# A weight ring with four double places: pairs of pieces in one 2 MB load, the rest in single places of 1 MB

## The chip, the cores and the metric

One core of one Trainium2 chip. The time is device microseconds of one execution of the whole program; the kernel before takes 1867.7 us (median of 3 runs, 1866.82 to 1869.79). "MB" of a weight piece below is 1024 KB, as in the profile's list of DMA issues; the profile's own sums of MB and its GB/s are decimal.

## The reference

A decoder block over 512 tokens of width 1024: a mixer (a state-space branch and a pooling branch, gated and merged), then a mixture of 32 experts of which every token takes four. The change touches the weights of the experts only. What an expert computes for its tokens:

```
def expert_block(args):
    xblk, e = args
    gu = xblk @ w_gu[e] + b_gu[e]
    glu, lin = jnp.split(gu, 2, axis=-1)
    glu = jnp.minimum(glu, SWIGLU_LIMIT)
    lin = jnp.clip(lin, -SWIGLU_LIMIT, SWIGLU_LIMIT)
    act = glu * jax.nn.sigmoid(SWIGLU_ALPHA * glu) * (lin + 1.0)
    return act @ w_down[e] + b_down[e]
```

`w_gu[e]` is 1024 x 2048 and `w_down[e]` 1024 x 1024 in f32: 8 MB and 4 MB of weights for each of 32 experts, each read once.

## The kernel before

The mixer runs until about 712 us, the experts from there to about 1846 us, and a short norm ends the program. The experts are taken in ranks of their token count, in an order that a host function (`order_of_ranks`) writes down; below, u is the place in that order. Experts with few tokens (u = 1, 2, then the even u from 4 to 24, and 30, 31) are "half": their products (`products`, L1106) multiply the raw weights (8 matmul records a piece in the trace). The others are "full": ACT and DVE split each half piece into a high and a low part (`esplit`, which calls the split at L117 and L118) and PE makes 6 matmuls of each half piece, 12 of a piece (L1111 to L1113).

The main loop (before the last lines printed below) does for each u: `up(u)`, the eight pieces of `w_gu`, and then `down(u-1)`, the four pieces of `w_down` of the expert before; biases, the activation's rows and their transposes, the gather of the next tokens' rows and the scatter of results (POOL) hang on hooks between the pieces. So from u = 4 to u = 25 a repeating cycle is: `up` of a half expert, `down` of a full one, `up` of a full one, `down` of a half one.

Each piece is 1 MB and comes by one DMA that SP issues (`fetch`, L771). `fetch` takes the first name of the list `ring`, allocates the next tile of that name and puts the name back at the end: a first-in first-out ring, with 11 places of 1 MB in the steady state (S0 S1 S4 S5 r0 r1 r2 Z bc0 S8 r4). Several of the places also serve the mixer before and the last norm after. SP takes its DMAs strictly in order: a load whose place is still being read stops SP, and all later loads with it, until the last reader (PE for a half expert, the splits on ACT and DVE for a full one) is done. The scheduler that orders the instructions may hoist a load as early on SP as its order allows. The host hands over `wgu` and `wdn`; a piece of `wgu` has runs of 8 KB in a partition, one of `wdn` two runs of 4 KB. The number of each expert is read from a table by `value_load` (L757, on SP).

Of the kernel before, what the change touches and what calls it, by code (L numbers as in the profile page):

```python
# [9 lines left out]
F32 = mybir.dt.float32  # L10
# [10 lines left out]
P = 128  # L21
D = 1024
# [4 lines left out]
NE = 32  # L27
# [41 lines left out]
def hybrid_block(ctx: ExitStack, tc: tile.TileContext, cst, cols, rows, xt, xf, wad0, wada, bada,  # L69
                 wx, wz, wdt, wu, wg, wso, wpl, wpo, wo, wr, ball, wgu, wdn, out):  # L70
    nc = tc.nc
    V, S, G, TE, SP = nc.vector, nc.scalar, nc.gpsimd, nc.tensor, nc.sync
    sb = ctx.enter_context(tc.tile_pool(name="sb", bufs=1))
    pm = ctx.enter_context(tc.tile_pool(name="pm", bufs=4, space=PSUM))
    dr = ctx.enter_context(tc.tile_pool(name="dr", bufs=1, space=DRAM))
    uid = [0]


    shared = dict(t1=0, t2=512, dt=1024, ac=1152, dte=1280, eac=1408, cdk=1536, cwh=1664, tri=1784)
    Z = sb.tile([P, 2048], F32, tag="Z", name="Z")  # L80

    def T_(tag, cols_, dt=F32, parts=P):
        if tag in shared:
            o = shared[tag]
            return Z[0:parts, o:o + cols_]
        uid[0] += 1
        return sb.tile([parts, cols_], dt, tag=tag, name=f"{tag}_{uid[0]}")

    def bank(tag="mm"):
        uid[0] += 1  # L90
        return pm.tile([P, 512], F32, tag=tag, name=f"{tag}_{uid[0]}")
# [233 lines left out]
    dt, negA, a2 = T_("dt", P), T_("negA", NH), T_("a2", 2 * P)  # L325
# [376 lines left out]
    for jj in range(4):  # L702
        whi, wlo = load_split(wg[4 + jj])
        for j in (2 * jj, 2 * jj + 1):
            t = gate(whi, wlo, j % 2)
# [22 lines left out]
    for j in range(KD):  # L728
        if j % 2 == 0:
            whi, wlo = load_split(wg[j // 2])  # L730
        t = gate(whi, wlo, j % 2)
# [9 lines left out]


    def weights(e):
        def of(w, lo_, hi_):
            return w[e, lo_:hi_, :] if isinstance(e, int) else w[bass.ds(e, 1), lo_:hi_, :].squeeze(0)

        return dict(wu=lambda k: of(wgu, k * P, (k + 1) * P), got={},
                    wd=lambda c: of(wdn, c * 256, (c + 1) * 256).rearrange("(k p) d -> p k d", p=P))

    order = order_of_ranks()  # L750
    big = order.index(NE - 1)
# [6 lines left out]
        return wts[u]  # L758


    ring, kept = ["bc0", "S4", "S5", "r0", "r1", "r2", "S7", "r3"], ["Z", "bc0", "S8", "r4"]
    nload = [0, 0]
    wsp = []

    def fetch(w, kind, k, t=None):
        if t is None:
            t = ring.pop(0)
            if t not in ("S7", "r3", "S3"):
                ring.append(t)
        r = T_(t, 2048)  # L770
        SP.dma_start(r if kind == "wu" else r.rearrange("p (k d) -> p k d", k=2), w[kind](k))  # L771
        return r

    def eload(w, kind, k):
        return w["got"].pop((kind, k), None) or fetch(w, kind, k)

    def esplit(r):
        if not wsp:
# [16 lines left out]
    ss2, r2 = T_("ss2", 2 * NB), T_("rst", NB)  # L795
# [50 lines left out]
    for n in range(2):  # L846
# [6 lines left out]
        for b in range(NB):  # L853
# [9 lines left out]
            t = xg_rot()  # L863
# [342 lines left out]

    def warm():
        S.activation(rf[0:64, 0:1], parts[0][0][1][0][:, 0:1].bitcast(F32), AF.Sqrt, scale=0.0, bias=eps1[0:64, :])
        f = T_(ring.pop(3), D)
        fin.extend([f[:, 0:512], f[:, 512:D]])  # L1210
        for n in range(2):
            dg, ps = g_rot(), bank("ss")
            for k in range(4):
                f = Q_FN + n * 4 + k
                V.tensor_scalar(dg[:, k * P:(k + 1) * P], ident, qc[:, f:f + 1], None, op0=ALU.mult)
            TE.matmul(ps, ones, dg, start=True, stop=True)
            S.activation(fin[n], ps, AF.Copy)
# [117 lines left out]
    turn_routing()  # L1335
    first_rows()
    fetch_down(2, 4)
    ring[:] = ["S0", "S1", "S3", "S4", "S5", "r0", "r1", "r2", "r3"]
    ahead.append(list(pieces(weights_of(0)["got"]["wu", 1], True)))
    xe2 = []  # L1340

# [8 lines left out]
    prev, parts, pend, begin = None, [], [], []  # L1350
    for u in range(NE + 1):
        hooks = {}
        if u < NE:
            w, sel = weights_of(u), sel_of(u)
            pre = {k: list(f) for k, f in extra.get(u, {}).items()}
            if u != 0:
                pre.setdefault(0, []).append(lambda: prep(u + 2))
            if u == big - 2:
                pre.setdefault(4, []).append(prep_x)
            if pend:  # L1360
                pre[1] = pend + pre.get(1, [])
                pend = []
            for n, f in enumerate(begin):
                pre[n] = [f] + pre.get(n, [])
            begin = []
            pss = up(xs_[u], sel, w, pre)
            aTs = [op_of(Rot(["q16"]) if u == 1 else a_rot, xs_[u][0].half)]
            hooks = {n: [f] for n, f in enumerate(acts(pss[0], aTs[0]))}
            if u == big:
                aTs.append(op_of(Rot(["b12"]), True))  # L1370
                lx = act_rows(*pss[1])
                hooks[0].insert(0, lambda: act_turn(lx, aTs[1], 0))
            hooks[2] = hooks.get(2, []) + [lambda: turned(u + 1)]
            if u >= FIXED:
                hooks[0] = hooks.get(0, []) + [lambda: select(u + 1)]
            if u == big - 1:
                hooks[3] = hooks.get(3, []) + [turned_x]
        if u == NE:
            hooks = {0: [warm, lambda: open_sums(0, 3)], 1: [lambda: open_sums(3, 5)], 2: [lambda: open_sums(5, 7)]}
        if prev is None:  # L1380
            ls = [act_rows(pss[0][n], pss[0][n + 2]) for n in range(2)]
            begin = [lambda n=n, l=l, a=aTs[0]: act_turn(l, a, n) for n, l in enumerate(ls)]
            turned(1)
        else:
            v, aT0 = prev
            if v == 0:
                ring.extend(kept)
            psd = down(aT0, sel_of(v), weights_of(v), hooks)
            if u >= NE - 1:
                parts.append(spread(psd[0], sts[v]))  # L1390
            else:
                send(psd[0], sts[v])
                if len(psd) > 1:
                    pend.append(lambda p=psd[1]: send(p, sts["x"], "q16"))
        if u < NE:
            prev = (u, aTs)

    t0t = [T_(ring.pop(0), 2048) for _ in range(2)]
    t0 = [t0t[b // 2][:, (b % 2) * D:(b % 2 + 1) * D] for b in range(NB)]
    for b in range(NB):  # L1400
        SP.dma_start(t0[b], y_d[b * P:(b + 1) * P, :])
# [26 lines left out]
    with tc.For_i(0, nov, 1) as i:  # L1428
        w = tabled(bass.ds(i, 1))
# [4 lines left out]
        x = turn(st, x_rot)  # L1434
# [40 lines left out]
def _layout(i):  # L1475
    A = np.ascontiguousarray

    def tiles(w):
        return w.reshape(KD, P, w.shape[1] // P, P).transpose(2, 1, 0, 3)

    def pairs(t):
        return t.reshape(-1, 2, P, 1024).transpose(0, 2, 1, 3).reshape(-1, P, 2048)

    def halves(w):
        n = w.shape[1] // 512
        return w.reshape(2, 4, P, n, 512).transpose(3, 0, 2, 1, 4).reshape(n, 2, P, 2048)

    x, w_in = i["x"][0], i["w_in"][0]
    fcol = lambda v: v.reshape(-1, P).T
    cols = np.concatenate([  # L1490
        i["conv_w"][0].reshape(4, 24, P).transpose(2, 1, 0).reshape(P, 96), fcol(i["conv_b"][0]),
        fcol(i["ssd_norm_w"][0]), fcol(i["pool_scale"][0]), fcol(i["norm_mix_w"][0]), fcol(i["c"][0]),
        fcol(i["norm_ffn_w"][0]), fcol(np.repeat(i["d_skip"][0], 64)),
        fcol(i["norm_final_w"]), fcol(i["b_ada"][0][:2048]).reshape(P, 2, 4, 2).transpose(0, 2, 1, 3).reshape(P, 16)], axis=1)
    rows = np.concatenate([i["a_log"][0], i["dt_bias"][0], i["b_router"][0]])
    order = [t for g in range(4) for t in (16 + g, 20 + g, 4 * g, 4 * g + 1, 4 * g + 2, 4 * g + 3)]
    d = dict(
        cst=_consts(), cols=A(cols), rows=rows,
        xt=A(x), xf=A(x.T.reshape(2, 4, P, T).transpose(0, 2, 1, 3).reshape(2, P, 2048)),
        wad0=A(i["w_ada"][0][:, :2048].reshape(2, 4, P, 2, 4, 256).transpose(4, 0, 2, 1, 3, 5).reshape(4, 2, P, 2048)), wada=A(halves(i["w_ada"][0][:, 2048:])), bada=A(i["b_ada"][0].reshape(12, 512)),  # L1500
        wx=A(pairs(tiles(w_in[:, 2048:5120])[order])),
        wz=A(pairs(tiles(w_in[:, 0:2048]))),
        wdt=A(w_in[:, 5120:5152].reshape(KD, P, NH).transpose(1, 0, 2).reshape(P, 256)),
        wu=A(pairs(tiles(w_in[:, 5152:6176]))),
        wg=A(pairs(tiles(w_in[:, 6176:8224]))),
        wso=A(i["w_ssd_out"][0].reshape(4, 4, P, 2, 4, P).transpose(0, 3, 2, 4, 1, 5).reshape(8, P, 2048)),
        wpl=A(i["w_pool"][0].reshape(4, 2, P, 256).transpose(2, 0, 1, 3).reshape(P, 2048)),
        wpo=A(pairs(tiles(i["w_pool_out"][0]))),
        wo=A(halves(i["w_out"][0]).reshape(4, P, 2048)),
        wr=A(i["w_router"][0].reshape(KD, P, NE).transpose(1, 0, 2).reshape(P, 256)),  # L1510
        ball=A(np.concatenate([i["b_gu"][0], i["b_down"][0]], axis=1).reshape(NE, 3, 2, 512).transpose(2, 0, 1, 3).reshape(2, NE, 1536)),
        wgu=A(i["w_gu"][0]), wdn=A(i["w_down"][0]))
    return d


# [17 lines left out]
```

## Time and profile before

| | |
|---|---|
| median of 3 runs | 1867.7 us (1866.82 to 1869.79) |
| the profiled execution, its own time | 1870.85 us |
| its span | 1869.1 us |
| granted TensorE clock, mean | 0.989 |
| PE busy | 1788.1 us, 96% of the span |
| HBM read | 502.89 MB |

The span is the time from the first to the last instruction of that one execution; the own time also holds what lies around it. PE is the engine that is nearly always busy; the question for a change of the loads is whether they still come before PE wants them.

### The profile page before, as it was taken

Reading aid. Unit: us, or ns where it says so; the run is one execution under the profiler, and the core shown is the slowest. Engines: PE = TensorE matmul, PEld = TensorE weight load, DVE = VectorE, ACT = ScalarE, POOL = GpSimd, SP = SyncE. Lnnn points to the kernel's source line nnn. Section 1 sums busy time; section 2 is a strip of 40 time slices with the busy share of each in tenths; the row PEclk is TensorE's granted clock in tenths of the full one; section 3 lists DMA queues with packets and bytes.
Section 4 is the critical chain, followed back from the end, with each engine's and each line's share of the span. In section 5 each row is a group of like instructions: output and inputs, shape, how many; then the busy total and the mean of one; then the engine's idle time right before and its main releaser. Section 6 shows DMA issues by size and latency. Waiting matters only on the chain. (4 is left out here: it accounts for less than half of the span.)

```text
span 1869.1 us, 23339 instructions
## 1 busy us (share of the span) xinstructions
PE 1788.1 (96%) x8353; PEld 1165.1 (62%) x8353; DVE 1213.9 (65%) x1803; ACT 947.0 (51%) x1458; POOL 220.0 (12%) x214
## 2 busy tenths in 40 slices
PE   6999999999999999999999999999999999999995
PEld 3787687867768777456456455455564565677741
DVE  5888685857574548657557566375675585799933
ACT  4433545536362346346455455264555455577822
POOL 0000000010100002121111111121112111211111
PEclk9999999999999999999999999999999999999998
DMA  8265233352443458999999998789999999989894
GB/s 349 76 251 221 90 135 113 113 134 93 124 130 136 178 218 296 371 402 400 388 373 402 380 366 326 305 309 373 382 402 377 380 403 364 397 327 341 316 365 191
DMA packets 102728, 527.81 MB, mean 282 GB/s; under 512 B 11737, under 2 KB 12377, under 8 KB 60368
## 3 DMA queue, kind: packets, MB, share of 16 engines
q1 hardware_dynamic: 90544, 498.14, 68.8%
q0 software_dynamic: 11184, 25.50, 6.4%
q10 hardware_dynamic: 880, 2.64, 0.4%
q8 instruction: 67, 1.10, 0.2%
q14 instruction: 53, 0.43, 0.1%
HBM read 502.89 MB, written 25.77 MB: 283 GB/s over the span
## 5 line engine op out<-in xcount | busy, mean ns | idle before, releaser
L118 DVE TENSOR_TENSOR wl<-r,wh 128x1024 fp32r<-128x1024 f32 x246 | 303.6, 1260 | 109.4 <-ACT wh L117 100.2
L117 ACT ACTIVATE wh<-r 128x1024 fp32r<-128x1024 f32 x246 | 253.9, 1057 | 136.3 <-PE mm L266 56.2
L118 DVE TENSOR_TENSOR wl<-S,wh 128x1024 fp32r<-128x1024 f32 x186 | 229.8, 1271 | 34.3 <-ACT wh L117 34.1
L1112 PE MATMUL mm<-wl,S 128*128 128x512 f32 x540 | 217.3, 402 | 9.7 <-DVE wl L118 9.0
L1113 PE MATMUL mm<-wh,S 128*128 128x512 f32 x540 | 214.5, 397 | 0.0
L117 ACT ACTIVATE wh<-S 128x1024 fp32r<-128x1024 f32 x186 | 189.5, 1055 | 47.5 <-PE mm L1113 34.9
L265 PE MATMUL mm<-S,wh 128*128 128x512 f32 x512 | 207.9, 407 | 4.0 <-ACT S L117 4.0
L267 PE MATMUL mm<-S,wl 128*128 128x512 f32 x512 | 206.3, 403 | 1.5 <-DVE wl L118 1.5
L266 PE MATMUL mm<-S,wh 128*128 128x512 f32 x512 | 206.5, 403 | 0.0
L1111 PE MATMUL mm<-wh,S 128*128 128x512 f32 x540 | 177.7, 402 | 8.0 <-ACT wh L117 8.0
L1147 DVE TENSOR_SCALAR q<-mm 128x512 f32<-128x512 f32 x49 | 32.9, 687 | 181.8 <-PE mm L1106 153.1
L1148 ACT ACTIVATE q<-q 128x512 f32<-128x512 f32 x50 | 31.3, 632 | 218.0 <-DVE q L1147 217.8
L1112 PEld LDWEIGHTS mm<-wl,S 128*128 128x128 f32 x540 | 102.2, 189 | 47.6 <-DVE wl L118 17.0
L1111 PEld LDWEIGHTS mm<-wh,S 128*128 128x128 f32 x540 | 100.6, 188 | 48.7 <-ACT wh L117 16.3
L265 PEld LDWEIGHTS mm<-S,wh 128*128 128x128 f32 x512 | 97.2, 190 | 33.0 <-issue 7.1
L1113 PEld LDWEIGHTS mm<-wh,S 128*128 128x128 f32 x540 | 102.4, 190 | 21.5
L267 PEld LDWEIGHTS mm<-S,wl 128*128 128x128 f32 x512 | 97.0, 190 | 29.7 <-issue 6.4
L266 PEld LDWEIGHTS mm<-S,wh 128*128 128x128 f32 x512 | 97.3, 190 | 26.9 <-issue 4.2
L1112 PE MATMUL ss<-wl,S 128*128 128x512 f32 x240 | 97.1, 405 | 1.9 <-DVE wl L118 1.5
L1106 PE MATMUL mm<-S,S 128*64 128x512 f32 x408 | 96.2, 596 | 0.0
L1172 POOL TENSOR_TENSOR y<-y,q 128x512 f32<-128x512 f32 x47 | 67.7, 1453 | 237.9 <-ACT y L1171 237.2
L1113 PE MATMUL ss<-wh,S 128*128 128x512 f32 x240 | 95.5, 398 | 0.0
(499 smaller groups left out, 3101.2 us busy)
## 6 DMA issues: line engine op xcount, KB each, us to landing
S<-in_wgu SPq DMA_DIRECT2D x113, 1024.0 KB, 9.6
r<-in_wgu SPq DMA_DIRECT2D x97, 1024.0 KB, 8.4
S<-in_wdn SPq DMA_DIRECT2D x61, 1024.0 KB, 11.7
r<-in_wdn SPq DMA_DIRECT2D x44, 1024.0 KB, 13.2
bc<-in_wgu SPq DMA_DIRECT2D x23, 1024.0 KB, 10.3
Z<-in_wgu SPq DMA_DIRECT2D x23, 1024.0 KB, 10.0
r<-in_wada SPq DMA_DIRECT2D x16, 1024.0 KB, 6.7
r<-in_wx SPq DMA_DIRECT2D x12, 1024.0 KB, 6.1
```

Source lines behind the costliest of these rows:

```text
L117: S.activation(hi, src, AF.Copy)
L118: V.tensor_tensor(lo, src, hi.bitcast(F32), op=ALU.subtract)
L265: TE.matmul(ps, a, hh(k), start=k == 0, stop=False)
L266: TE.matmul(ps, a, hl(k), start=False, stop=False)
L267: TE.matmul(ps, b, hh(k), start=False, stop=k == KD - 1)
L1106: TE.matmul(rows_of(ps, n0 + i), x.c[k], hl[:, o + i * 512:o + (i + 1) * 512], start=False, stop=stop)
L1111: TE.matmul(p, x.h[k], h, start=False, stop=False)
L1112: TE.matmul(p, x.h[k], l, start=False, stop=False)
L1113: TE.matmul(p, x.l[k], h, start=False, stop=stop)
L1147: V.tensor_scalar(g, pg, LIM, None, op0=ALU.min)
L1148: S.activation(t, g, AF.Tanh, scale=ALPHA / 2)
L1172: G.tensor_tensor(yn, yn, gaf2[0] if half else gaf[n], op=ALU.mult)
```

## The change

The host lays the weights out anew, outside the timed program: two neighbouring pieces of `wgu` (and of `wdn`) stand side by side, 16 KB in a partition. On the chip the ring gets four double places, R0 = S0 + S1, R1 = S4 + S5, R2 = r0 + r1 and R3 = r2 + Z, each one tile of 128 x 4096. `fetch` now takes the first place of the ring that suits: a double place only for a piece with even k, and then one DMA of 2 MB brings pieces k and k + 1; a single place (S3, r3 at the start, then bc0, S8, r4) brings one piece of 1 MB. The memory in the ring stays 11 MB: four double places and three single ones. The mixer's tiles S0 to Z become halves of the same double tiles.

```
+    pairs_of = dict(S0=("R0", 0), S1=("R0", 1), S4=("R1", 0), S5=("R1", 1), r0=("R2", 0), r1=("R2", 1), r2=("R3", 0), Z=("R3", 1))
+    twos = {}
+
+    def new_pair(name, dt=F32):
+        uid[0] += 1
+        twos[name] = (sb.tile([P, 4096], dt, tag=name, name=f"{name}_{uid[0]}"), dt, set())
+        return twos[name][0]
...
+        if tag in pairs_of:
+            name, h = pairs_of[tag]
+            if name in ("R0", "R1") and (name not in twos or h in twos[name][2] or twos[name][1] != dt):
+                new_pair(name, dt)
+            twos[name][2].add(h)
+            return twos[name][0][0:parts, h * 2048:h * 2048 + cols_]
...
     def fetch(w, kind, k, t=None):
         if t is None:
-            t = ring.pop(0)
+            t = ring.pop(next(i for i, x in enumerate(ring) if k % 2 == 0 or x not in twos))
             if t not in ("S7", "r3", "S3"):
                 ring.append(t)
-        r = T_(t, 2048)
-        SP.dma_start(r if kind == "wu" else r.rearrange("p (k d) -> p k d", k=2), w[kind](k))
-        return r
+        if t not in twos:
+            r = T_(t, 2048)
+            SP.dma_start(r, w[kind](k, 1))
+            return r
+        r = new_pair(t)
+        SP.dma_start(r, w[kind](k, 2))
+        w["got"][kind, k + 1] = r[:, 2048:4096]
+        return r[:, 0:2048]
...
-    ring[:] = ["S0", "S1", "S3", "S4", "S5", "r0", "r1", "r2", "r3"]
+    ring[:] = ["R0", "S3", "r3", "R1", "R2"]
...
             if v == 0:
-                ring.extend(kept)
+                ring.extend(["R3"] + kept[1:])
```

What this gives in the steady state, on SP, where all the loads are issued: the loads of `down(6)` (a half expert), `up(8)` (half) and the first of `down(7)` (full). The names are places of the ring with the number of the tile; the queue semaphore and the last reader stand behind "waits"; the row ISA that stands ahead of each DMA is left out. Before, each load takes the place that was read longest ago; the twelfth load after S1_973 is the first that takes its place again:

```order
L771 DMA S1_973_7108<-in_wdn 128x2x1024 [waits DMAHW4_49,DVE_49]
L771 DMA S4_978_7132<-in_wdn 128x2x1024 [waits DMAHW5_49,DVE_49]
L771 DMA S5_983_7153<-in_wdn 128x2x1024 [waits DMAHW6_49,DVE_49]
L771 DMA r0_986_7173<-in_wdn 128x2x1024 [waits DMAHW7_49,DVE_49]
L771 DMA r1_990_7198<-in_wgu 128x2048 [waits DMAHW0_49,DVE_49]
L771 DMA r2_996_7233<-in_wgu 128x2048 [waits DMAHW1_49,DVE_49]
L771 DMA S0_1001_7263<-in_wgu 128x2048 [waits DMAHW6_49,DVE_49]
L771 DMA S1_1002_7269<-in_wgu 128x2048 [waits DMAHW7_49,PE_49]
L771 DMA S4_1006_7280<-in_wdn 128x2x1024 [waits DMAHW0_49,PE_49]
```

(Z, bc0, S8 and r4 stand between r2_996 and S0_1001.) The same loads with the change:

```order
L791 DMA r4_866_6973<-in_wdn 128x2048 [waits DMAHW2_49,DVE_49]
L791 DMA bc0_871_6997<-in_wdn 128x2048 [waits DMAHW3_49,DVE_49]
L791 DMA S8_876_7018<-in_wdn 128x2048 [waits DMAHW4_49,DVE_49]
L791 DMA r4_879_7038<-in_wdn 128x2048 [waits DMAHW1_49,PE_49]
L794 DMA R0_883_7063<-in_wgu 128x4096 [waits DMAHW5_49,DVE_49]
L794 DMA R1_889_7102<-in_wgu 128x4096 [waits DMAHW6_49,DVE_49]
L794 DMA R2_890_7112<-in_wgu 128x4096 [waits DMAHW7_49,DVE_49]
L794 DMA R3_891_7122<-in_wgu 128x4096 [waits DMAHW0_49,DVE_49]
L791 DMA bc0_895_7137<-in_wdn 128x2048 [waits DMAHW2_49,PE_49]
```

What moved: every `up` now takes the four double places and every `down` the three single ones, so that the fourth piece of a `down` (r4_879) takes the place of the first piece of the same `down` (r4_866), and waits for PE, its reader; the four double loads of the next `up` stand behind it on SP.

On ACT, around the start of `down(7)` (full): q6 and q4 are rows of the activation of the half expert 8 (tanh), wh the high part of a split, S2 the gathered rows of a later expert. Before:

```order
L1074 ACTIVATE q11_1016_7362<-mm_1017_7363,colf_67_388 128x128 x3
L117 ACTIVATE S2_1013_7349<-q11_1016_7362 128x512 [waits Activation_49]
L1148 ACTIVATE q6_1008_7299<-q4_1007_7298 128x512 [waits DVE_49]
L117 ACTIVATE wh1_713_5236<-S4_1006_7280 128x1024 [waits DMAHW0_49]
L1157 ACTIVATE r1_1003_7275<-ss_1005_7306 128x512 [waits PE_49]
```

With the change:

```order
L1099 ACTIVATE q11_905_7219<-mm_906_7220,colf_64_384 128x128 x3
L135 ACTIVATE S2_902_7206<-q11_905_7219 128x512 [waits Activation_49]
L135 ACTIVATE wh1_633_5155<-bc0_895_7137 128x1024 [waits DMAHW1_49]
L1173 ACTIVATE q6_897_7156<-q4_896_7155 128x512 [waits DVE_49]
L135 ACTIVATE wh0_632_5154<-S8_900_7170 128x1024 [waits DMAHW2_49]
```

What moved: the splits of the first piece of `down(7)` stand ahead of the tanh of expert 8, and PE takes that piece's matmuls right behind `up(8)`, ahead of the transposes of expert 8's activation.

One more thing moves on SP: with the change 28 of the 31 table reads (`value_load`, L775 there) stand in one row between the loads S3 and r3 of expert 1; before, one stood ahead of each expert's first load.

## Rows read from the trace of the kernel before

**Rows 1.** The page, parts 1 and 2: busy time; DMA share in 40 slices.
```profile
PE 1788.1 (96%) x8353; PEld 1165.1 (62%) x8353; DVE 1213.9 (65%) x1803; ACT 947.0 (51%) x1458; POOL 220.0 (12%) x214
DMA  8265233352443458999999998789999999989894
```

**Rows 2.** Waits of PE and its weight loads, 866 to 1140 us: total, times, longest.
```profile
PE mm L1112 <- DVE wl L118: 3.8, 5, 0.9
...
PEld ss L1106 <- DMA S<-in_wgu: 1.1, 3, 0.4
```

**Rows 3.** Waits of SP's DMA queue, 866 to 1140 us: total, times, longest.
```profile
SPq L771 <- DVE wl L118: 103.9, 43, 6.3
SPq L771 <- PE ss L1106: 46.6, 12, 5.5
```

**Rows 4.** Two cycles: length; busy PE, PEld, DVE, ACT, POOL; clock, DMA share, GB/s.
```profile
866.58:934.64 68.06, 65.20 (x299) 37.92 (x297) 42.37 (x57) 36.03 (x52) 11.09 (x11) 1.00 1.01 392
934.64:1002.50 67.86, 65.11 (x298) 37.93 (x297) 42.23 (x57) 36.02 (x52) 10.59 (x10) 1.00 0.98 381
```

**Rows 5.** DMA queues, 934 to 1002 us: packets, MB, share of 16 engines.
```profile
q1 hardware_dynamic: 4438, 24.85, 91.5%
q0 software_dynamic: 432, 1.00, 6.3%
```

**Rows 6.** DMA issues: median us to landing, 1154 to 1187 us, then 750 to 1850 us.
```profile
r<-in_wgu SPq DMA_DIRECT2D x3, 1024.0 KB, 4.7
...
S<-in_wgu SPq DMA_DIRECT2D x103, 1024.0 KB, 10.0
```

**Rows 7.** PE's timeline, 958 to 1003 us: start, length, operation, count.
```profile
960.41 1.93 PE L1106 MATMUL ss<-S,r 128*64 128x512 f32 x6
...
973.36 1.94 PE L1106 MATMUL mm<-r,S 128*64 128x512 f32 x8
...
984.39 3.60 PE L1106 MATMUL mm<-S,S 128*64 128x512 f32 x16
...
990.41 0.71 PE L1111 MATMUL ss<-wh,S 128*128 128x512 f32 x2
...
1002.50 0.62 PE L1111 MATMUL mm<-wh,S 128*128 128x512 f32 x2
```

**Rows 8.** SP's timeline, 961 to 975 us: the load into S1_973's place.
```profile
962.38 0.33 SPq L771 DMA_DIRECT2D S<-in_wgu  x1
```

**Rows 9.** DVE's and ACT's splits by line, 750 to 1850 us: busy, mean ns.
```profile
L118 DVE TENSOR_TENSOR wl<-S,wh 128x1024 fp32r<-128x1024 f32 x180 | 222.2, 1271 | 33.0 <-ACT wh L117 32.7
...
L117 ACT ACTIVATE wh<-S 128x1024 fp32r<-128x1024 f32 x180 | 183.2, 1055 | 46.9 <-PE mm L1113 34.3 <-PE ss L1113 10.7 <-DVE wl L118 1.1
```

**Rows 10.** PE and SP around the start of up(3) and the release of down(1).
```profile
799.31 0.39 PE L1111 MATMUL mm<-wh,S 128*128 128x512 f32 x1
799.54 0.40 PE L1112 MATMUL mm<-wl,S 128*128 128x512 f32 x1
...
790.72 0.33 SPq L771 DMA_DIRECT2D Z<-in_wgu  x1
```

**Rows 11.** SP and PE in the run of full experts, 25 to 29.
```profile
1646.46 0.33 SPq L771 DMA_DIRECT2D S<-in_wgu  x1
...
1656.88 0.71 PE L1111 MATMUL mm<-wh,S 128*128 128x512 f32 x2
```

**Rows 12.** SP and PE at the end: last places released, up(31).
```profile
1794.46 6.96 SPq L771 DMA_DIRECT2D S<-in_wgu  x3
...
1820.54 5.32 PE L1106 MATMUL mm<-S,S 128*64 128x512 f32 x24
```

**Rows 13.** SP's table reads (L757, ns); SP's and PE's timeline in expert 1.
```profile
L757 SPq TENSOR_LOAD <-eidi x31: 262/273/657, 712.3 to 1783.5; - x31
...
727.21 10.68 SPq L771 DMA_DIRECT2D r<-in_wgu  x4
...
750.91 3.65 PE L1106 MATMUL mm<-S,y 128*64 128x512 f32 x16
```

More of the change, by code (lines that the diff above doesn't have):

```diff
@@ L79, in hybrid_block @@
     shared = dict(t1=0, t2=512, dt=1024, ac=1152, dte=1280, eac=1408, cdk=1536, cwh=1664, tri=1784)
-    Z = sb.tile([P, 2048], F32, tag="Z", name="Z")
+    pairs_of = dict(S0=("R0", 0), S1=("R0", 1), S4=("R1", 0), S5=("R1", 1), r0=("R2", 0), r1=("R2", 1), r2=("R3", 0), Z=("R3", 1))
[4 more added lines that the diff above has]
+        return twos[name][0]
+    for n in ("R2", "R3"):
+        new_pair(n)
     def T_(tag, cols_, dt=F32, parts=P):
         if tag in shared:
-            o = shared[tag]
-            return Z[0:parts, o:o + cols_]
+            o = 2048 + shared[tag]
+            return twos["R3"][0][0:parts, o:o + cols_]
+        if tag in pairs_of:
[4 more added lines that the diff above has]
+            return twos[name][0][0:parts, h * 2048:h * 2048 + cols_]
         uid[0] += 1
@@ L743, in weights, with of @@
     def weights(e):
[L744 to L748, printed above, removed]
+        def of(w, i, n):
+            r, c = slice(i // 2 * P, (i // 2 + 1) * P), slice(i % 2 * 2048, (i % 2 + n) * 2048)
+            return w[e, r, c] if isinstance(e, int) else w[bass.ds(e, 1), r, c].squeeze(0)
+        return dict(wu=lambda k, n: of(wgu, k, n), wd=lambda c, n: of(wdn, c, n), got={})
     order = order_of_ranks()
@@ L766, in fetch @@
         if t is None:
-            t = ring.pop(0)
+            t = ring.pop(next(i for i, x in enumerate(ring) if k % 2 == 0 or x not in twos))
             if t not in ("S7", "r3", "S3"):
                 ring.append(t)
-        r = T_(t, 2048)
-        SP.dma_start(r if kind == "wu" else r.rearrange("p (k d) -> p k d", k=2), w[kind](k))
-        return r
+        if t not in twos:
[6 more added lines that the diff above has]
+        return r[:, 0:2048]
     def eload(w, kind, k):
-        return w["got"].pop((kind, k), None) or fetch(w, kind, k)
+        g = w["got"].pop((kind, k), None)
+        return fetch(w, kind, k) if g is None else g
     def esplit(r):
@@ L1208, in warm @@
         S.activation(rf[0:64, 0:1], parts[0][0][1][0][:, 0:1].bitcast(F32), AF.Sqrt, scale=0.0, bias=eps1[0:64, :])
-        f = T_(ring.pop(3), D)
+        f = T_(ring.pop(next(i for i, x in enumerate(ring) if x not in twos)), D)
         fin.extend([f[:, 0:512], f[:, 512:D]])
@@ L1396, in hybrid_block @@
             prev = (u, aTs)
-    t0t = [T_(ring.pop(0), 2048) for _ in range(2)]
+    t0p = new_pair(ring.pop(next(i for i, x in enumerate(ring) if x in twos)))
+    t0t = [t0p[:, i * 2048:(i + 1) * 2048] for i in range(2)]
     t0 = [t0t[b // 2][:, (b % 2) * D:(b % 2 + 1) * D] for b in range(NB)]
@@ L1511, in _layout @@
         ball=A(np.concatenate([i["b_gu"][0], i["b_down"][0]], axis=1).reshape(NE, 3, 2, 512).transpose(2, 0, 1, 3).reshape(2, NE, 1536)),
-        wgu=A(i["w_gu"][0]), wdn=A(i["w_down"][0]))
+        wgu=A(i["w_gu"][0].reshape(NE, 4, 2, P, 2 * D).transpose(0, 1, 3, 2, 4)).reshape(NE, 4 * P, 4 * D), wdn=A(i["w_down"][0].reshape(NE, 2, 4, P, D).transpose(0, 1, 3, 2, 4)).reshape(NE, 2 * P, 4 * D))
     return d
```

## The prediction

> **What bounds the kernel now.** I read the page first: PE is busy for 96% of the span [rows 1], and the DMA engines, lightly used in the mixer, are at seven to nine tenths through the experts, which are slices 16 to 39 of 40 (same rows). So both are candidates in the part that the change touches. The waits tell them apart. Over four cycles of experts (866 to 1140 us) PE's longest total is 3.8 us, for splits; for a weight load its weight loads waited 1.1 us in three times [rows 2]. SP on the other hand waits for places to come free, 103.9 us for DVE's splits and 46.6 us for PE [rows 3]. So the loads are ahead of PE and the ring is full: **PE bounds, with the DMA engines close behind**. How close is read from the windows of two cycles: 68.06 and 67.86 us, DMA share 1.01 and 0.98 [rows 4]. In the second one the weight queue moved 24.85 MB, which is 24.85/1.0486 = 23.7 pieces of 1 MB, at a share of 91.5%, while POOL's gathers and scatters took 6.3% [rows 5]. A piece therefore costs 0.915 x 67.86/23.7 = 2.62 us of all engines by itself, and 67.86/23.7 = 2.86 us with what runs beside it. I take **2.75 us a piece**, between them. A load that finds the engines idle lands after 4.7 us; where the queue is full the median is 10.0 us [rows 6]. So some 4.7 - 2.7 = 2.0 us pass before or after the data, and the rest is queue.
>
> What the change can cost thus hangs on one question: does the DMA stream stay unbroken? Before, the load that needs the first place of `down(6)` is the last piece of `up(8)`, and of `up(8)` seven pieces are already issued by then. PE finished that place at about 962.3 us [rows 7] and SP issued the load at 962.38 [rows 8].
>
> **The change, part by part.**
>
> *The wait of the fourth down piece.* With the change the fourth piece of each `down` takes the place of its own first piece, and the 8 MB of the next `up` stand behind it. So at 962.38 us, when `down(6)`'s first piece has been read, nothing but its second and third piece is on the chip, and nine pieces remain to be moved before the last pair of `up(8)` can start. They land at 962.38 + 2.0 + 9 x 2.75 = 989.1 us. PE took the last pair's 16 matmuls at 984.39 and finished at 987.99 [rows 7]: 4.7 us late.
>
> What is late next? `down(7)`'s first piece lands 2.75 us on, at 991.9. Its first half needs ACT's part (1055 ns) and DVE's (1271 ns) [rows 9], 2.3 us, but the first matmuls take the high part alone, some 0.4 us earlier: PE could start at about 993.7 against 990.41 [rows 7], 3.3 us late. So 1.4 us of the 4.7 come back: PE stood 2.4 us between `up(8)` and `down(7)`, with little but biases and transposes in it, and in the new order that piece's matmuls come ahead of the transposes. Then `up(9)`. From the last pair of `up(8)` to its first pair there are six pieces (`down(7)`'s four and the pair): 989.1 + 6 x 2.75 = 1005.6, and with 1.9 us of split 1007.5, where PE began it at 1002.50 [rows 7]: **5.0 us late**. This is the later of the two chains, so it sets the cycle. The fourth piece of `down(7)` does not break the stream: the splits of its first piece end 2 x 1.27 + 1.06 = 3.6 us after it lands, at 995.5, while the second and third piece land until 997.4. Behind the first pair of `up(9)` the pairs come every 5.5 us, and PE needs about 5.5 us for each (24 matmuls, 799.54 - 799.31 = 0.23 us apart [rows 10]), so nothing more is lost, and nothing is won back: what PE was behind stays, since the next release is again PE's reading of a `down` piece. There are eleven such cycles (`up` of the half experts 4, 6, ... 24): 11 x 5.0 = **+55 us**.
>
> *The same at the start.* Before `up(3)`, `down(1)`'s first place came free at 790.72 and PE began `up(3)` at 799.31 [rows 10]. Three pieces must land: 790.72 + 2.0 + 8.25 + 1.9 = 802.9, **+3.6**.
>
> *The run of full experts, 25 to 29.* There the place comes free when the splits are done, one piece into a `down` that PE works on for four: 1646.46 + 2.0 + 8.25 + 1.9 = 1658.6 against 1656.88 [rows 11]: 1.7 us in each of four such changeovers, **+7**.
>
> *The end.* `up(31)`, a half expert behind a full `down(29)`: the last of three releases came at 1794.46 + 6.96 = 1801.4; nine pieces land at 1801.4 + 2.0 + 24.75 = 1828.2, where PE, 5.32/3 = 1.8 us a piece, began the last pair at 1820.54 + 1.8 = 1822.3 [rows 12]: 5.9. `up(30)`, likewise, I put at 2, since its release comes earlier against its end. Together **+8**.
>
> *Edits at nothing.* About 128 fewer DMA issues on SP: SP waits over 150 us of 274 for places [rows 3], so its own time is hidden. The 4 KB runs that become 8 and 16 KB: inside the 2.62 us; bounded below. The 28 table reads moved into expert 1: 0.27 to 0.66 us each [rows 13], 8 to 18 us on SP ahead of its fourth piece; four loads were issued there from 727.21 to 737.89, PE wanted the fourth piece at 750.91 (same rows), and the load needs 4.7. By 18 us it would land at 727.2 + 18 + 4.7 = 749.9, just in time; if the cover were gone, a few us once. In the mixer a double tile is free only when both halves are: DMA share is 2 to 5 tenths there [rows 1], so I take 0, with 5 as the upper end.
>
> *Sum.* 55 + 3.6 + 7 + 8 = 74 us on the profiled execution's own 1870.85: 1945. That execution stands 3.15 above the median of the runs, so against the runs **1942 us**.
>
> *The unknown size: time per piece.* Fifteen pieces lie in the chain of a cycle. At 2.62 us it gives 5.0 - 15 x 0.13 = 3.0 a cycle, 33 in all, and with the smaller terms 47: 1915. At 2.86 it gives 6.6, 73 in all, and 96 with the rest: 1964. The change lays the runs longer, and the two bounds hold other traffic of POOL than the new stream will meet; I stay between, which is nearest to both rows.
>
> The Trainium skill ("DMA: Bandwidth & Descriptors", section "Anatomy of one DMA") fits a DMA of the GpSimd path as 2.0 us plus bytes at 436 GB/s. By this a 2 MB load would take 6.8 us against 8.8 us for two of 1 MB, and the change would be a gain. The trace agrees with the 2.0 us for a load alone [rows 6], but back to back a piece took 2.62 to 2.86 us, not 4.4 [rows 5]: here the fixed part overlaps, unless a wait breaks the stream, and the change adds such a break to each cycle.
>
> **The rivals.**
>
> *Hidden by the reserve.* The ring holds 11 MB before and after, so the stream may stay ahead as it was. For it: PE waits nearly nowhere for a load [rows 2]. Against: in the order of SP all of the next `up` stands behind a wait for the `down` before, so only two pieces are in reserve at that moment. It would hold if `down`'s first piece were read much earlier than the row shows. Then 1868 us, no change.
>
> *Faster: the bigger loads are cheaper a byte.* The fixed part of a load may not overlap wholly, and 2 MB loads then take less per MB. The cycle's 5.0 us vanish when fifteen pieces save 5.0 us: 2.75 - 0.33 = 2.42 us a piece. Below that the new order on PE would give its 1 us of the gap at 987.99 in each of eleven cycles, 11 us: 1857. Against it: the bare share gives 2.62 [rows 5], so the pure transfer would have to be quicker by 8%, with POOL's traffic free.
>
> *Slower still: ACT's order.* ACT now holds `down(7)`'s first split, which waits for its DMA, ahead of the tanh of expert 8. That DMA lands at 991.9 where ACT was free from about 988: activations and the transposes behind them come some 4 us later, and PE, in order, may stand another 2 us a cycle. It decides where this exceeds the 1.7 us between the two chains above. With 2.86 us a piece and 2 more in each cycle: 1964 + 22 = 1986.
>
> **How the numbers follow.** About 0.2% (3.7 us) can be told from no change here. The forecast case, a stream broken once a cycle at 2.5 to 2.86 us a piece, has 0.82; hidden 0.03; faster 0.04; slower still 0.11. By sign: faster 0.04, same 0.04 (the hidden case and the edge of the forecast's low end), slower 0.92. The range takes the two bounds, 1915 and 1964, and goes below to 1900 (2.53 us a piece, if longer runs help) and above to the case of ACT's order, 1985.
>
> **What would show it.** Right: PE waits in the chain for DMA into R0 to R3 at `up` of half experts and for splits of R0 at `up` of full ones; a cycle of 71 to 75 us instead of 68; DMA share in it 0.90 to 0.95, with an empty stretch of some 3 us behind each half `down`'s third piece; on SP the load of the fourth `down` piece ends on PE's reading of the first, with four double loads at its heels. Wrong: cycles of 68 us with no such wait (hidden), a stretch of double loads at 2.4 us a MB (cheaper), or PE's waits naming ACT or POOL rather than DMA.

## The result, and the profile after

The changed kernel takes 1944.25 us (median of 4 runs, 1940.36 to 1955.33) against 1868.1 us (4 runs, 1866.82 to 1869.79): 1.0416 times as long, 95% interval 1.0391 to 1.044. Forecast were 1942 us and slower. The profiled execution took 1940.36 us with a span of 1938.3, which is 69.2 us more than the span before.

The page, parts 1, 2 and 6, for the changed kernel:

```profile
PE 1783.8 (92%) x8352; PEld 1161.4 (60%) x8353; DVE 1220.7 (63%) x1803; ACT 947.2 (49%) x1458; POOL 236.2 (12%) x214
...
DMA  8265132353552668798988986789889989888895
...
R<-in_wgu SPq DMA_DIRECT2D x123, 2048.0 KB
```

PE does the same work (1783.8 us against 1788.1 in [rows 1]) in a longer span, and the DMA row, which stood at 9 through most of the experts, is now mixed with 8s: both engines have gaps. Where the time went is found by cutting both traces at PE's first product of an `up` (the start is read in PE's timeline):

| stretch | before | after | difference | forecast |
|---|---|---|---|---|
| mixer, to `up(0)` | 715.5 | 709.9 | -5.6 | 0 (to +5) |
| `up(0)` to `up(3)` | 83.8 | 88.4 | +4.6 | +3.6 |
| `up(3)` to `up(25)`, eleven cycles | 780.3 | 841.5 | +61.2 | +55 |
| `up(25)` to `up(30)`, full experts | 199.4 | 200.2 | +0.8 | +7 |
| `up(30)` to the end of `down(31)` | 67.5 | 74.5 | +7.0 | +8 |

Nearly all of it lies in the eleven cycles, on average 5.6 us in each (1.6 to 7.7). One of them, `up(13)` to `up(15)`, holds a larger expert and takes 96.8 us before and 98.4 after; the others take 67 to 71 us before. The windows view shows the last ten of them, `up(5)` to `up(25)`, in one row (columns as in [rows 4]); before:

```profile
866.58:1579.63 713.05, 686.73 (x3090) 385.98 (x3089) 432.35 (x582) 365.65 (x522) 118.42 (x105) 1.00 0.97 370
```

and after:

```profile
871.64:1639.73 768.09, 689.39 (x3090) 386.99 (x3090) 438.19 (x583) 365.94 (x522) 133.22 (x105) 0.98 0.87 344
```

55.0 us more at the same PE work, the DMA share down from 0.97 to 0.87. PE's waits in these stretches say on what (line and operation, what ended the wait: total, times, longest). Before:

```profile
PE ss L1066 <- DVE q L111: 7.4, 9, 0.8
PE mm L1112 <- DVE wl L118: 7.3, 10, 0.9
PE mm L1111 <- ACT wh L117: 5.8, 16, 0.5
```

After:

```profile
PE mm L1131 <- DMA R<-in_wgu: 36.5, 21, 3.3
PE mm L1136 <- ACT wh L135: 19.0, 18, 2.4
PE mm L1125 <- ACT q L1099: 11.3, 9, 1.3
PE mm L1137 <- DVE wl L136: 5.8, 9, 0.8
```

The two that were forecast are there: raw double places for `up` of a half expert (36.5 us), splits of a double place for `up` of a full one (19.0). The third, 11.3 us for rows of ACT (L1099), was not forecast; it stands between the release and the start of a half `up`.

One cycle step by step, the one of the prediction (`down(6)`, `up(8)`, `down(7)`, `up(9)`). SP's timeline: start, time from the first to the last issue of the group, line, what, count.

```profile
972.61 0.33 SPq L791 DMA_DIRECT2D r<-in_wdn  x1
973.18 2.30 SPq L794 DMA_DIRECT2D R<-in_wgu  x4
...
1008.49 0.33 SPq L791 DMA_DIRECT2D bc<-in_wdn  x1
1009.07 2.23 SPq L794 DMA_DIRECT2D R<-in_wgu  x4
```

Each time a single load, the fourth piece of a `down`, and right on its heels the four double loads of the next `up`: they had stood behind it. What the DMA engines did meanwhile is in the view of the DMA, 964 to 984 us, in 40 slices of half a microsecond:

```profile
DMA  9999888640000000000979899999999989999989
GB/s 426 410 442 459 377 377 344 279 197 33 33 16 0 0 0 0 0 0 0 229 180 295 344 393 442 541 393 459 426 459 393 393 360 459 459 426 492 426 360 426
```

From 968.5 to 973.5 they are all but idle: 5 us, all loads done, the next ones blocked on SP until 972.61. PE's timeline shows the price:

```profile
994.41 3.65 PE L1131 MATMUL mm<-R,S 128*64 128x512 f32 x16 [1.87 <-DMA R<-in_wgu]
1000.11 5.35 PE L1131 MATMUL mm<-R,S 128*64 128x512 f32 x16 [2.04 <-DMA R<-in_wgu]
```

The last pair of `up(8)` starts 1000.11 - 972.61 = 27.5 us after the release; before it was 984.39 - 962.38 = 22.0 [rows 7, 8]. Behind the wait the same 16 matmuls take 5.35 us instead of 3.65: part of them ran at the lower of the clock's two levels (the granted clock of this stage is 0.92; its row stands further below).

### The profile page after: what moved, and what is told of

It reads as the page before. It is cut to its first block, busy times and chain, and to the rows that moved or that the text cites. A ratio compares the mean times of both kernels' runs of the same rounds, so it can differ in the third digit from the quotient of the medians.

```text
span 1938.3 us, 22696 instructions
## 1 busy us (share of the span) xinstructions
PE 1783.8 (92%) x8352; PEld 1161.4 (60%) x8353; DVE 1220.7 (63%) x1803; ACT 947.2 (49%) x1458; POOL 236.2 (12%) x214
## 5 line engine op out<-in xcount | busy, mean ns | idle before, releaser
L136 DVE TENSOR_TENSOR wl<-R,wh 128x1024 fp32r<-128x1024 f32 x364 | 445.1, 1264 | 159.0 <-ACT wh L135 149.9
L135 ACT ACTIVATE wh<-R 128x1024 fp32r<-128x1024 f32 x364 | 372.6, 1057 | 187.7 <-PE mm L284 56.2
L1131 PE MATMUL mm<-R,S 128*64 128x512 f32 x896 | 215.6, 623 | 46.9 <-DMA R<-in_wgu 46.9
L1136 PE MATMUL mm<-wh,S 128*128 128x512 f32 x540 | 195.4, 408 | 26.6 <-ACT wh L135 26.6
L283 PE MATMUL mm<-R,wh 128*128 128x512 f32 x512 | 206.5, 404 | 4.1 <-ACT R L135 4.1
L285 PE MATMUL mm<-R,wl 128*128 128x512 f32 x512 | 205.0, 401 | 1.5 <-DVE wl L136 1.5
L284 PE MATMUL mm<-S,wh 128*128 128x512 f32 x512 | 205.5, 401 | 0.0
L1136 PEld LDWEIGHTS mm<-wh,S 128*128 128x128 f32 x540 | 99.8, 190 | 71.4 <-ACT wh L135 39.6
L283 PEld LDWEIGHTS mm<-R,wh 128*128 128x128 f32 x512 | 96.4, 188 | 32.9 <-issue 6.8
L285 PEld LDWEIGHTS mm<-R,wl 128*128 128x128 f32 x512 | 96.3, 188 | 29.3 <-issue 6.4
L284 PEld LDWEIGHTS mm<-S,wh 128*128 128x128 f32 x512 | 96.5, 188 | 26.6 <-issue 4.2
L135 ACT ACTIVATE wh<-S 128x1024 fp32r<-128x1024 f32 x48 | 48.8, 1054 | 87.9 <-DMA S<-in_wdn 74.0
L1136 PE MATMUL ss<-wh,S 128*128 128x512 f32 x240 | 81.9, 402 | 1.2 <-ACT wh L135 1.2
```

Source lines behind the costliest of these rows:

```text
L135: S.activation(hi, src, AF.Copy)
L136: V.tensor_tensor(lo, src, hi.bitcast(F32), op=ALU.subtract)
L283: TE.matmul(ps, a, hh(k), start=k == 0, stop=False)
L284: TE.matmul(ps, a, hl(k), start=False, stop=False)
L285: TE.matmul(ps, b, hh(k), start=False, stop=k == KD - 1)
L1131: TE.matmul(rows_of(ps, n0 + i), x.c[k], hl[:, o + i * 512:o + (i + 1) * 512], start=False, stop=stop)
```

## The experiments

Ten kernels. Each differs from the change, or from the kernel before where that is said, by the edit shown; `...` marks lines left out.

**One double load ahead of the fourth piece.** In `down(2)` to `down(29)` the next `up`'s first double load is issued before the fourth `down` piece; the rule by which `fetch` takes a place is spelled out so that `up` keeps the double places and `down` the single ones.

```
+    def down(aTs, sel, w, hooks, nxt=None, first=0):
...
+            for k in range(0, 2 * first if c == 3 else 0, 2):
+                nxt["got"]["wu", k] = fetch(nxt, "wu", k)
             r = eload(w, "wd", c)
...
-            t = ring.pop(next(i for i, x in enumerate(ring) if k % 2 == 0 or x not in twos))
+            t = ring.pop(next(i for i, x in enumerate(ring) if ((x in twos) == (kind == "wu") if steady else k % 2 == 0 or x not in twos)))
...
-            psd = down(aT0, sel_of(v), weights_of(v), hooks)
+            go = 2 < u < NE - 1
+            steady[:] = [u] if go else []
+            psd = down(aT0, sel_of(v), weights_of(v), hooks, weights_of(u + 1) if go else None, (1) if go else 0)
```

> The change with one line of order altered: from down(2) to down(29), the next up's first double load is issued ahead of the down's fourth piece, all else alike. Theory (the stream stops because the fourth down piece takes the place of the first, with all double loads behind it): only seven pieces stand behind the stop instead of nine, so up of a half expert gets its last pair about 5.4 us sooner, and the first pair of the next full expert no longer waits for that stop at all. The loss goes: 1862 to 1880 us. Rival (2 MB loads, their landing as one, or the new layout cost the time by themselves): still over 1915 us.

Measured: 1883.53 us, 1.0075 times before (1.0058 to 1.0092). The same 2 MB loads, places and layout, and four fifths of the loss (61 of 76 us) are gone by one load standing elsewhere in SP's order. It lies 3.5 us above the range that was expected; the ten cycles take 720.4 us, 0.7 a cycle more than before, and the mixer of the profiled execution was 4.5 us longer than before's, of which more below.

```profile
872.77:1593.14 720.37, 683.03 (x3091) 384.58 (x3089) 429.23 (x584) 366.74 (x522) 127.92 (x105) 1.00 0.92 366
```

**Two double loads ahead, everywhere.** The same with `first` = 2.

> As the run before, with two double loads ahead of the fourth down piece. Theory: the stream never stops, 1860 to 1885 us; against one pair ahead it can only lose what the fourth piece itself comes late in a full down (it then has 4 MB ahead of it), 0 to 10 us. Rival: over 1915 us.

Measured: 1917.65 us, 1.026 (1.0243 to 1.0277). Missed: faster than the change, but 34 us behind one pair ahead, where 0 to 10 were allowed for. What it says is told with the two halves of this edit, which follow.

**Two double loads ahead in half downs only.**

```
+            psd = down(aT0, sel_of(v), weights_of(v), hooks, weights_of(u + 1) if go else None, (2 if aT0[0].half else 0) if go else 0)
```

> Two double loads ahead of the fourth piece in the downs of half experts only. The prediction on record has the loss in this stop alone: about 1870 us. The theory after reading the trace has two stops in a cycle, the second in the down of the full expert, whose first piece is read 5.6 us after it lands and not 3.6: then the first pair of the next up still comes some 16 us after that down begins where before it needed 12, 2 to 4 us a cycle remain, and with the run of full experts 1890 to 1912 us.

**Two double loads ahead in full downs only.** The same with `0 if aT0[0].half else 2`.

> Two double loads ahead of the fourth piece in the downs of full experts only. By the prediction on record the stop in a full down costs nothing, so nothing changes: 1935 to 1950 us. By the theory with two stops the last pair of a half up still comes 4 to 5 us late, but the next full up then begins only some 1.7 us late and PE wins that back in the down behind it: 1868 to 1895 us.

Measured: half downs 1892.56 us, 1.0129 (1.0112 to 1.0146); full downs 1977.08 us, 1.0576 (1.0558 to 1.0594), slower than the change itself and outside both expected ranges. The first total is what the theory with two stops asked for, but the trace does not bear that theory out. Half downs only, ten cycles, windows and PE's waits:

```profile
874.03:1590.93 716.90, 679.36 (x3090) 399.60 (x3090) 430.49 (x583) 366.36 (x522) 124.35 (x105) 0.99 0.93 369
```

```profile
PE mm L1136 <- ACT wh L135: 18.5, 17, 2.2
PE mm L1125 <- ACT q L1099: 12.1, 9, 1.4
```

The cycles take 716.9 us, 0.4 a cycle more than before, though PE's wait for splits at the start of a full `up`, the mark of the second stop, is all there: 18.5 us as against 19.0. So beside that wait next to nothing is lost, and the stop in the half down is nearly the whole loss in the cycles. Of the 24 us that this kernel is behind, only 3.8 are in these cycles; 4.3 lie before `up(3)`, whose stop the edit does not reach, 2.7 in `up(3)` to `up(5)`, 9.2 behind `up(30)`.

In full downs the edit is a new wait. SP's and PE's timelines of that kernel:

```profile
1007.62 4.34 SPq L794 DMA_DIRECT2D R<-in_wgu  x2
1026.07 0.33 SPq L791 DMA_DIRECT2D bc<-in_wdn  x1
```

```profile
1042.00 1.22 PE L1136 MATMUL ss<-wh,S 128*128 128x512 f32 x2 [3.45 <-ACT wh L135]
```

The two double loads, 4 MB, are in the queue of the DMA engines before the fourth piece is issued at 1026.07; PE waits for its split until 1042.00. The first of the two, issued at 1007.62, landed only at 1031.68 in the trace, so both were still ahead of the fourth piece when that was issued. In the ten cycles PE waits 21.9 us for such splits (`ss`, L1136); with two ahead everywhere it is 17.1 us, and that run's miss goes with it. Here, a load issued ahead of one that was wanted sooner made that one late.

**One double load ahead in full downs only**, so that the new wait is small and the second stop can be judged by itself.

> As the run with full downs only, but with one double load ahead of the fourth piece in them, not two, so that this piece has 2 MB and not 4 MB ahead of it; the stop in half downs stays. If the stop in the half down is what sets the cycle (27 us from it to the last pair, whatever the full down does), most of the loss stays: 1915 to 1945 us. If either stop is enough to lose the time and either cure enough to get it back: 1880 to 1900 us.

Measured: 1937.65 us, 1.0363 (1.0333 to 1.0393), in the first of the two ranges. Windows and waits of its ten cycles:

```profile
871.58:1640.06 768.48, 693.85 (x3090) 381.83 (x3089) 439.62 (x584) 367.62 (x522) 134.26 (x105) 0.99 0.86 343
```

```profile
PE mm L1131 <- DMA R<-in_wgu: 36.6, 20, 3.0
PE mm L1137 <- DVE wl L136: 16.1, 26, 1.4
...
PE mm L1136 <- ACT wh L135: 2.7, 13, 0.3
```

The mirror image: the wait at the start of a full `up` is gone (2.7 us for the high parts), the wait for raw pairs is as it was (36.6), and the cycles take 768.5 us, as in the change (768.1). PE has not stopped waiting for splits, though: its wait for the low parts, in the same `up`, is 16.1 us where the change has 5.8. Together with the half downs alone, where the wait at the start is all there and the cycles are short, and with the next run, which eases both stops, this settles it: **the stop in the half down sets the cycle, the stop in the full down does not.**

**Two ahead in half downs, one in full downs.**

> Two double loads ahead in half downs, one in full downs. If the stop in the full down costs something of its own, this is faster than two in half downs alone (1892.6): 1870 to 1882 us. If it is won back within the cycle, as that run's starts of up suggest (0.4 us a cycle), no gain there: 1885 to 1896 us.

Measured: 1882.8 us, 1.007 (1.0046 to 1.0095), between the two expectations, 10 us better than half downs alone. The ten cycles take 720.2 us, no better (716.9): won back within the cycle, as expected.

```profile
864.96:1585.16 720.20, 680.79 (x3091) 389.72 (x3090) 433.52 (x584) 366.61 (x522) 127.17 (x105) 1.00 0.94 367
```

The gain lies outside: in `up(3)` to `up(5)` (64.2 us against 70.0) and from `up(30)` to the end (70.8 against 76.7), places that the expectation left out.

**Double places loaded in halves.** Two loads of 1 MB into the two halves of the same double place.

```
-        SP.dma_start(r, w[kind](k, 2))
+        for i in range(2):
+            SP.dma_start(r[:, i * 2048:(i + 1) * 2048], w[kind](k + i, 1))
```

> The change with each double load issued as two loads of 1 MB into the halves of the same double place; places, order and layout as in the change. Theory: the stop stays and the last piece lands as late as before, so most of the loss stays; what goes is the wait for a whole pair where a full up begins (about 2.5 us in each of 11 cycles) and part of the last pair's PE time in a half up: 1905 to 1930 us. Rival (the 2 MB load itself is what costs): 1862 to 1880 us.

**The layout alone**, in the kernel before; the host's new layout and the reading of it in `weights` are as in the change.

```
...
-        SP.dma_start(r if kind == "wu" else r.rearrange("p (k d) -> p k d", k=2), w[kind](k))
+        SP.dma_start(r, w[kind](k))
...
```

> The kernel before with the new layout of the weights and nothing else: ring of 11 places of 1 MB, pieces now in runs of 8 KB for down as well as up. Theory: the layout is not what costs; within 5 us of before, 1860 to 1873 us. Rival (reading every second 8 KB of a 16 KB run is slower from memory): 1885 us or more.

**The places alone**, in the kernel before: its layout and its 1 MB loads.

```
+    two = dict(R0=("S0", "S1"), R1=("S4", "S5"), R2=("r0", "r1"), R3=("r2", "Z"))
+    second = {}
...
-            t = ring.pop(0)
+            t = second.pop((kind, k), None)
+            if t is None:
+                t = ring.pop(next(i for i, x in enumerate(ring) if k % 2 == 0 or x not in two))
...
+                if t in two:
+                    t, second[kind, k + 1] = two[t]
...
-    ring[:] = ["S0", "S1", "S3", "S4", "S5", "r0", "r1", "r2", "r3"]
+    ring[:] = ["R0", "S3", "r3", "R1", "R2"]
...
```

> The kernel before, with its layout and its 1 MB loads, but with the places given out as in the change: an up takes the eight places S0 to Z, a down takes bc0, S8, r4, so that a down's fourth piece takes the place of its first. Theory: the same two stops, less the wait for a whole pair: 1910 to 1935 us, clearly slower than before though no 2 MB load is in it. Rival (double loads or layout cost the time): 1868 us.

Measured: halves 1925.85 us, 1.0297 (1.027 to 1.0325); layout 1869.85 us, 1.0004 (0.9991 to 1.0018); places 1928.73 us, 1.0315 (1.0288 to 1.0342). All three as the theory had it. Neither double loads nor layout are needed for the loss: the order of the places takes 60 of the 76 us by itself. The window of its ten cycles, and PE's waits in them:

```profile
875.97:1625.52 749.55, 695.08 (x3091) 379.38 (x3089) 434.94 (x584) 366.82 (x523) 130.93 (x104) 1.00 0.91 353
```

```profile
PE mm L1113 <- DMA r<-in_wgu: 23.1, 24, 2.1
...
PE mm L1113 <- DMA Z<-in_wgu: 7.3, 10, 1.4
```

PE waits for the last pieces of a half `up`, in the r places and Z, with 1 MB loads too. The rest, some 16 to 18 us, comes with the double loads: the kernel with halves takes 748.8 us for the ten cycles, 1.9 a cycle less than the change.

```profile
877.18:1625.97 748.79, 694.41 (x3089) 379.05 (x3090) 435.67 (x583) 366.24 (x523) 131.29 (x104) 1.00 0.90 353
```

That it is the landing as one is not shown: in both kernels with 1 MB loads ACT takes the tanh of expert 8 ahead of the splits of `down(7)`, as before the change (halves: 1006.82 us, then 1007.43), so the two differ from the change in that order as well.

**The places given out in another pattern.** From `up(2)` on, an `up` takes three double and two single places, a `down` the fourth double place and two single ones.

```
-            t = ring.pop(next(i for i, x in enumerate(ring) if k % 2 == 0 or x not in twos))
+            t = ring.pop(next(i for i, x in enumerate(ring) if ((x in twos) == (k < (6 if kind == "wu" else 2)) if steady else k % 2 == 0 or x not in twos)))
...
+            if u == 2:
+                steady.append(u)
```

> The same four double and three single places, 2 MB loads and layout, but given out in another pattern from up(2) on: an up takes three double places and two single ones, a down the fourth double place and two single ones. The fourth down piece then waits for the place of the up's seventh piece, which PE reads one piece before the up ends, with three free double places behind it. Theory: this stop lies early enough that no load comes late; 1860 to 1876 us, the same as before. Rival (2 MB loads cost something by themselves, for example through later release of a place): 1885 us or more.

Measured: 1913.21 us, 1.022 (1.0192 to 1.0249): missed. The ten cycles, by the windows view:

```profile
874.06:1621.67 747.61, 695.06 (x3089) 400.33 (x3089) 444.49 (x583) 371.63 (x522) 139.94 (x104) 0.96 0.90 353
```

No wait for a weight load is among PE's larger ones any more, so far the theory holds. But the granted clock is 0.96 where before had 1.00, and the DMA share 0.90: there still is a stop (the DMA engines are all but idle from 1032 to 1037 us), and the cycles are 3.5 us longer. In `down(7)` the clock was 0.83, and matmuls stood 0.43 us apart instead of 0.23 for a while, after PE had stood in several short waits for DVE:

```profile
1002.35:1017.64 15.29, 13.97 (x49) 10.41 (x49) 9.65 (x11) 8.71 (x10) 7.13 (x4) 0.83 1.00 386
```

By the window rows PE is busy 8.3 us longer in the ten cycles than before, at the same count of matmuls, and idle 26.2 us longer: most of the loss is waits, not the clock. What brings these waits was not tried, and stays open. None of the ten kernels is faster than the one before.

## Why the prediction was right, point by point

**The bound, and where the stop is: right.** A wait on SP with 8 MB behind it empties the DMA engines in each cycle, and the kernel with the places alone shows that it is the place that matters.

**The first chain: right, in size too.** Forecast were 2.0 + 9 x 2.75 = 26.75 us from the release to the last pair; measured 27.5. Late by 5.5 us where 4.7 were forecast. With the same 2.0 us a piece took (27.5 - 2.0)/9 = 2.83 us, inside the two bounds, 2.62 and 2.86, and near the upper one.

**"The fourth piece of `down(7)` does not break the stream": wrong.** The step took the splits of its first piece as 3.6 us from landing. ACT and DVE at that place, in the changed kernel:

```profile
1002.57 2.00 ACT L135 ACTIVATE wh<-bc 128x1024 fp32r<-128x1024 f32 x2 [14.58 <-DMA bc<-in_wdn]
```

```profile
1004.65 0.69 DVE L1172 TENSOR_SCALAR q<-mm 128x512 f32<-128x512 f32 x1 [15.93 <-PE mm L1131]
1005.51 0.69 DVE L1174 TENSOR_SCALAR q<-mm 128x512 f32<-128x512 f32 x1 [0.17 <-PE mm L1131]
1006.12 2.35 DVE L136 TENSOR_TENSOR wl<-bc,wh 128x1024 fp32r<-128x1024 f32 x2
```

ACT begins as the piece lands. DVE, in order, has two rows of the activation of expert 8 ahead of its part, and these wait for PE's end of `up(8)`; so it starts 3.6 us after ACT and ends at 1008.47, and SP issues the fourth piece at 1008.49, 5.9 us after ACT's start. The prediction reckoned with ACT's order, not with DVE's. So the stream breaks a second time in the cycle; the view of the DMA, 1000 to 1020 us, has the engines idle from 1006 to 1009:

```profile
DMA  9999999999720000003979899999999999989193
```

Two of the signs that were named fell outside: the stretches without data are 5 and 3 us, not one of some 3, and the DMA share in the ten cycles is 0.87, not 0.90 to 0.95. The first pair of `up(9)` came late by more than the 5.0 us of the sum: 1022.04 against 1002.50 is 19.5, of which 10.2 were there at the release (972.61 against 962.38), so 9.3.

**"Nothing is won back": wrong as well, the other way.** From the start of `up(9)` to PE's reading of `down(8)`'s first piece it is 25.96 us after and 29.20 before. The windows of the three stages, `up(8)`, `down(7)`, and `up(9)` with that piece, before:

```profile
973.36:990.41 17.05, 15.82 (x71) 5.28 (x71) 4.03 (x7) 4.81 (x9) 2.89 (x2) 1.00 0.99 366
990.41:1002.50 12.09, 12.09 (x65) 9.61 (x64) 11.24 (x17) 7.80 (x10) 1.68 (x3) 1.00 1.02 386
1002.50:1031.70 29.20, 27.68 (x106) 19.45 (x104) 22.87 (x22) 17.29 (x19) 4.94 (x4) 0.94 1.02 408
```

and after:

```profile
984.88:1005.73 20.85, 16.94 (x68) 5.11 (x67) 2.30 (x4) 4.62 (x9) 2.04 (x2) 0.92 1.00 404
1005.73:1022.04 16.31, 13.26 (x67) 9.73 (x65) 12.17 (x20) 9.05 (x12) 1.58 (x2) 1.00 0.79 292
1022.04:1048.00 25.96, 25.06 (x105) 18.39 (x106) 23.38 (x23) 16.34 (x17) 7.90 (x4) 1.00 0.82 329
```

Before, `up(9)` had its own short waits for splits and a clock of 0.94 behind them; after, it starts later, its splits are ready ahead of it and the clock is 1.00. So +3.8 and +4.2 in the first two stages meet -3.2 in the third; another +1.3 lies between the release and `up(8)`, where PE waits 1.26 us for ACT (L1099). The two errors nearly cancel: release to release, this cycle is 75.4 us against 69.4, and the mean over the eleven is +5.6 where +5.0 were forecast. The sum set the cycle by the start of the full `up`, 5.0 us late, and the runs with half or full downs alone show that this start does not count: what carries the cost is the lateness of the last pair of the half `up`, 4.7 us in the prediction, with the low clock behind it. That the total is so close is luck in part: +6 in the cycles meets -6 in the run of full experts, and another -6 in the mixer that is not the change's.

**The smaller terms.** The start, +4.6 for +3.6, is right. The run of full experts was mis-sized: +0.8 for +7. The five experts in turn take 3.5 and 1.8 us more, then 0.7, 0.5 and 3.3 less; why the last three gain was not tried. The end has +7.0 for +8; its release was read 0.3 us late, since the 6.96 us of that row run to the end of the third issue.

**Edits at nothing.** The layout: 1.0004, shown. The table reads on SP: the two loads around them stand 731.93 - 709.06 = 22.9 us apart,

```profile
709.06 0.34 SPq L791 DMA_DIRECT2D S<-in_wgu  x1
731.93 0.33 SPq L791 DMA_DIRECT2D r<-in_wgu  x1
```

but 6.8 us of that are a wait of SP for DVE; the reads themselves take 16, inside the 8 to 18 forecast. And `up(1)` and `up(2)` start as far behind `up(0)` as before (to 0.4 us): covered. The mixer was taken at 0 and came out 5.6 us shorter; below.

**The rivals.** *Hidden by the reserve* fell by the wait itself. *Cheaper big loads*: not cheaper a MB. ACT began on one double load as it landed, at 1026.66 us, and on the next at 1031.56: 4.9 us for 2 MB. PE began on a double load as it landed, at 1000.11, and ACT on the single one behind it at 1002.57: 2.5 us for 1 MB. The DMA engines were busy some 0.87 x 768 = 668 us in the ten cycles against 0.97 x 713 = 692 before, but with 1 MB loads in the same places it is 0.90 x 749 = 674, so most of the difference is not the size of the load. The Trainium skill's fit for a DMA of the GpSimd path ("DMA: Bandwidth & Descriptors", "Anatomy of one DMA"), by which the change had to gain, gives an estimate of 4.4 us for 1 MB; here a load that finds the engines idle comes near it (4.7 us [rows 6]), one behind another does not. *ACT's order*: the three kernels with loads ahead in the half downs and one or none in the full ones keep the change's order on ACT and lose 0.4 to 0.7 us a cycle, not 2. It was DVE's order that held a place, and PE won that back.

## What to carry to other kernels

In a queue that issues in order, as SP's does here, a ring is only as deep as the number of loads ahead of the first one that must wait; count that, not the megabytes. When places of two sizes share a ring, write down for every load whose place it takes and how late that place is read: a load that takes the place of something read just before it stops all that stands behind. And a wait that shows up in the profile is not yet a cost: of the two new waits that were forecast, curing the one of 36.5 us gave back 51 us of the ten cycles, and curing the one of 19.0 us gave back nothing: PE met another wait behind it.

## What had not been expected

**The mixer's length varies by 10 us between executions of the same code.** The change and seven of the experiments share the mixer's code, and PE began `up(0)` at 709.9, 711.1, 712.6, 714.0, 715.9, 716.5, 718.5 and 720.0 us. One place where executions part is a store to memory that ACT waits for, before a block of the state-space branch; before:

```profile
410.29 0.60 ACT L661 ACTIVATE y<-mm 128x512 f32<-128x512 f32 x1 [7.19 <-DMA ys_d<-y]
```

where the change had

```profile
408.87 0.60 ACT L679 ACTIVATE y<-mm 128x512 f32<-128x512 f32 x1 [5.36 <-DMA ys_d<-y]
```

Behind it PE stood 2.78 us before and 0.95 after, and only before did matmuls then run 0.43 us apart for some 3 us. These two are different kernels, but with the change's mixer the same wait was 6.4 to 7.6 us in five of the experiments; and the kernel with the layout alone, which has the mixer of before, began `up(0)` at 710.3 us, not at 715.5. The 5.6 us by which this part was shorter are therefore not put down to the change. Why the store takes longer was not tried.
